# Attention tiles ordered by grid column, value windows loaded one grid row at a time, and four activation casts moved behind key copies

## The chip, the core and the metric

The kernel runs on one core of a Trainium2 chip. A core has a matrix engine (PE, with its weight loads shown apart as PEld), a vector engine (DVE), a scalar engine (ACT), a general engine (POOL) and a queue engine (SP), which work side by side and meet at semaphores. On-chip memory (SBUF) has 128 partitions; PE writes into a smaller memory, PSUM, from which DVE and ACT read. Sixteen DMA engines move data between SBUF and the chip's main memory. DMAs are issued here by SP and, in a few places, by ACT; each of the two works through its list in order, so an issue that has to wait holds up everything behind it.

The metric is the device time of one execution in microseconds (us). The time before is 1057.92 us, the median of three runs between 1056.41 and 1058.7.

## What is computed

One encoder layer over 1024 tokens of 1024 channels in float32. The tokens form a grid of 16 rows and 64 columns. The part that the change touches is the neighbourhood attention: each token attends to a window of 8 rows and 16 columns that is clamped inside the grid, with a learned bias per offset.

```python
h = rms_norm(x, norm1_g[l])
z = h @ w_in[l]
a, gate, q, k, v = jnp.split(z, splits, axis=-1)
conv_out = conformer_conv(a, gate, dw_kernel[l], dw_bias[l], conv_ln_g[l], conv_ln_b[l])
q = rms_norm(q.reshape(B, S, N_HEADS, HEAD_DIM), q_norm_g[l])
k = rms_norm(k.reshape(B, S, N_HEADS, HEAD_DIM), k_norm_g[l])
attn_out = neighbourhood_attention(q, k, v, rpb[l])
x = x + jnp.concatenate([conv_out, attn_out], axis=-1) @ w_out[l]
h = rms_norm(x, norm2_g[l])
x = x + (jax.nn.silu(h @ w_gate[l]) * (h @ w_up[l])) @ w_down[l]
```

There are 8 heads of 64 channels. The convolution has 31 taps over the token positions, for each of 512 channels, then a normalisation over channels and a silu.

## The kernel before

All instructions are written out in Python in the order in which each engine is to run them; no scheduler moves them. The framework adds the semaphore waits that the data need, and gives the SBUF buffers: 22 of kind `G` (128 x 1024), 6 of kind `H` (128 x 4096), 3 of kind `R` (raw weights). PSUM has four banks `mm`, two banks `tp` (mostly for transposes) and a double bank `cv`.

**Products.** A float32 product is made of three matmuls in a reduced format (`mac`, lines 113 to 117): each operand is split into a rounded part (a cast on ACT, line 107) and the rest (a subtraction on DVE or POOL, line 111).

**Start.** The input comes transposed, in two halves of 512 tokens. `h_split` (lines 273 to 277) makes the two parts of one 128-channel block of a half: a cast on ACT (276) and a difference on DVE (277). The keys of the first four tiles of 128 tokens are computed first (`four`, 524 to 528). `head_post` (437 to 445) squares, sums and scales a tile and then puts three entries into the list `woven`: two empty ones and one that does `head_T`. After four tiles the list has twelve entries, with the transposes at places 2, 5, 8 and 11. `weave` takes one entry off that list after each block of three matmuls, so these steps are issued between matmuls of the next product. `head_T` (403 to 413) transposes a scaled tile on PE into a `tp` bank and has ACT copy it out: to `kT` for keys (413), to `qT` for queries (411, two instructions). Between the fourth key tile and the first product of the convolution's gate, `glu_step(0, 0, 0, accs)`, lines 558 and 559 call `h_split` for the blocks 0 to 3 of the second half; lines 562 and 563 call it for the blocks 4 to 7 after that product. The first product that reads the second half is `glu_step(0, 1, 0, accs)` on line 571.

**Middle.** Gate and value of the convolution, the remaining keys and the queries follow; the 31 taps run on DVE (336) with some on ACT and POOL beside PE's products. Meanwhile SP builds six bias tables in main memory (`bias_tables`, 477 to 510), laid out as [i, j, head, column], where i is one of 8 grid rows and j one of 16 columns of a query tile.

**Attention.** A query tile is a block of 8 rows and 16 columns; there are 2 x 4 of them, named by the row half `rh` and the column block `cb`, and a tile's partition is 16 i + j. `order` (617) takes the column blocks 0, 3, 1, 2, each with both halves. Values are written to main memory by token (`value_out`, 417 to 420, issued by ACT). `load_vw` (608 to 613) then loads, for one column block, four grid rows of the columns that its windows can reach (24 or 32) into half of a `G` buffer, so that partition r x columns + c holds row r, column c. Four such loads make a window. `table` (592 to 603) loads a bias table with one partition per query. The loop from line 808 on does two pairs of heads in each of its steps: scores on PE (629), bias and maximum on DVE (641), exponential on ACT (646), scaling on POOL (657), transposes on PE (665), copies on DVE and ACT (670), weighted sums of the values on PE (681). It also issues loads: the table of the middle column blocks for row half 0 at step 4, the window of block 1 at step 6, the table of row half 1 at step 8, the window of block 2 at step 12. Two tables share `H` buffers with older ones. Ahead of the loop stand the windows of blocks 0 and 3 and the last of the first four tables (lines 719 to 728).

SP has eight semaphores for its DMAs and uses them in turn, so an issue also waits until the DMA eight before it has landed.

**After attention.** The output of the convolution is transposed, normalised and split into `cm` by `conv_silu` (777 to 783), where its tokens are put into the order of the attention tiles. From here to the end a tile of 128 tokens is such a block. `rows` (785 to 787) is the view that gives a block's tokens in the input and in the output: `load_x2` (789) loads the residual with it, and `store` (1221 to 1224) writes the result with it. Output projection, norm, and the feed-forward part follow; the latter uses seven products of half-size blocks in place of eight, and its last four partial results are summed on DVE (1246) and stored by ACT's queue.

Of the kernel before, what the change touches and what calls it, by code (L numbers as in the profile page):

```python
# [8 lines left out]
AF = mybir.ActivationFunctionType  # L9
# [15 lines left out]
GW = 64  # L25
# [36 lines left out]
def body(tc, a):  # L62
    from contextlib import ExitStack
    with ExitStack() as ctx:
        build(ctx, tc, a)


def build(ctx, tc, a):
    nc = tc.nc
    pe, act, dve, pool = nc.tensor, nc.scalar, nc.vector, nc.gpsimd  # L70
# [5 lines left out]
    def T(tag, shape, bufs, name, dt=F32):  # L76
        return sb.tile(shape, dt, tag=tag, bufs=bufs, name=name)

    def G(name, dt=F32):
        return T("G", [P, 1024], 22, name, dt)  # L80
# [4 lines left out]
    def H(name, dt=F32):  # L85
        return T("H", [P, 4096], 6, name, dt)
# [13 lines left out]
    def tp(name):  # L100
        return ps.tile([P, 512], F32, tag="tp", bufs=2, name=name)
# [4 lines left out]
    def split(hi, lo, src, sub=(pool,)):  # L106
        act.copy(hi, src)  # L107
        n = src.shape[-1] // len(sub)
        for i, eng in enumerate(sub):
            sl = slice(i * n, (i + 1) * n)  # L110
            eng.tensor_tensor(*[w[..., sl] for w in (lo, src, hi.bitcast(F32))], OP.subtract)  # L111
# [11 lines left out]
    woven = []  # L123
# [94 lines left out]
    FIRST, SECOND, ALL = slice(0, 256), slice(256, 512), slice(0, 512)  # L218
# [33 lines left out]
    for _ in range(11):  # L252
# [3 lines left out]
    qgs = T("qgs", [P, 1], 1, "qgs")  # L256
    dve.tensor_scalar(qgs, qg, HD ** -0.5, None, op0=OP.mult)
    t1 = [dr.tile([NH, 16, 15, ncol], F32, name=f"t1{ty}") for ty, ncol in enumerate((24, 32, 24))]
    tf = {(rh, ty): dr.tile([8, 16, NH, AR * t1[ty].shape[-1]], F32, name=f"tf{rh}{ty}")
          for rh in range(2) for ty in range(3)}  # L260
# [12 lines left out]
    def h_split(h, k, sl):  # L273
        src = xr[h, k // 2][:, k % 2, sl]
        hi, lo = [w[:, k, sl] for w in hT[h]]
        act.activation(hi, src, AF.Copy, scale=g1[:, k:k + 1])
        dve.scalar_tensor_tensor(lo, src, g1[:, k:k + 1], hi.bitcast(F32), OP.mult, OP.subtract)
# [101 lines left out]
    qT, kT = H("qT").rearrange("p (c s) -> p c s", s=S), H("kT").rearrange("p (c s) -> p c s", s=S)  # L379
# [23 lines left out]
    def head_T(n, t, zn):  # L403
        pt = tp(f"zt{n}{t}")
        for c in range(4):
            pe.transpose(pt[:, c * P:(c + 1) * P], zn[:, c * P:(c + 1) * P], ident)
        if n == 0:
            q5 = qT.rearrange("p c (h b i j) -> p c h b i j", h=2, b=4, j=16)
            p5 = pt.rearrange("p (c i b j) -> p c i b j", c=4, i=2, j=16)
            for i in range(2):  # L410
                act.activation(q5[:, :, t // 4, :, 2 * (t % 4) + i, :], p5[:, :, i], AF.Copy, scale=qgs)
        else:
            act.activation(kT[:, :, t * P:(t + 1) * P], pt.rearrange("p (c s) -> p c s", s=P), AF.Copy, scale=kg)

    vd = dr.tile([S, 512], F32, name="vd")
# [21 lines left out]
    def head_post(n, t, z, lag=7):  # L437
        def f(n_taps):
            sd = head_sq(n, t, z)
            pump(2 + {(1, 5): 3, (0, 1): 2}.get((n, t), 0))  # L440
            zn = head_scale(n, t, z, sd)
            pump(1)
            woven.extend([lambda: None] * lag)
            woven.append(lambda: head_T(n, t, zn))
        return f
# [109 lines left out]
    take(1)  # L555
    r_rows(0)
    head_post(1, 3, zs[3], 2)(4)
    for k in range(4):
        h_split(1, k, ALL)
    accs = {}  # L560
    glu_step(0, 0, 0, accs)
    for k in range(4, KB):
# [28 lines left out]

    def table(rh, ty):
        n = AR * t1[ty].shape[-1]
        src = tf[rh, ty].rearrange("i j h c -> (i j) (h c)")
        if rh == 0 and ty == 0:
            parts = [(G(f"tab{k}")[:, :n * min(3, NH - 3 * k)], 3 * k) for k in range(3)]
        else:
            parts = [(H(f"tab{rh}{ty}")[:, :NH * n], 0)]
        heads = []
        for w, h0 in parts:  # L600
            nc.sync.dma_start(w, src[:, h0 * n:h0 * n + w.shape[-1]])
            heads += [w[:, o:o + n] for o in range(0, w.shape[-1], n)]
        return heads


    vwt, vw = {}, {}

    def load_vw(cb, g):
        c0, ncol, _ = WIN[cb]
        if g % 2 == 0:  # L610
            vwt[cb, g // 2] = G(f"vw{cb}{g}").rearrange("p (g d) -> p g d", d=512)
        vw[cb, g] = vwt[cb, g // 2][:4 * ncol, g % 2, :]
        nc.sync.dma_start(vw[cb, g], vd.rearrange("(r c) d -> r c d", c=GW)[g * 4:g * 4 + 4, c0:c0 + ncol, :])


    k4 = kT.rearrange("p c (r w) -> p c r w", w=GW)
# [3 lines left out]
    def score_mm(i):  # L620
        s_, hp = divmod(i, 4)
        rh, cb = order[s_]
        t = rh * 4 + cb
        c0, ncol, _ = WIN[cb]
        s2 = cv(f"s{i}") if i > 0 and i % 2 == 0 else None
        out = []
        for hh in range(2):
            s = (mm(f"s{i}{hh}") if s2 is None else lr(s2)[hh])[:, :AR * ncol]
            pe.matmul(s, qT[hh * HD:(hh + 1) * HD, hp, t * P:(t + 1) * P],  # L629
                      k4[hh * HD:(hh + 1) * HD, hp, rh * 4:rh * 4 + AR, c0:c0 + ncol], start=True, stop=True)  # L630
            out.append(s)
        return out
# [62 lines left out]
    def value(t):  # L695
        z = nat(2, t)
        step(lambda n_taps: (value_out(t, z), pump(n_taps)))
# [1 line left out]
    jobs = []  # L699

    def load_window(cb):
        for g in range(4):
            load_vw(cb, g)

    for t in range(6):
        value(t)
        if t == 2:
            while aside_dma:
                behind()
            tab[0, 0] = table(0, 0)  # L710
        if t == 3:
            tab[1, 0] = table(1, 0)
            tab[0, 3] = table(0, 2)
# [2 lines left out]
    both(0, s0)  # L716
    pump(200)
    value(6)
    for g in range(3):
        load_vw(0, g)  # L720
    s1 = score_mm(1)
    value(7)
    score_norm(0)
    both(1, s1)
    step()
    load_vw(0, 3)
    load_window(3)
    tab[1, 3] = table(1, 2)


    xd = dr.tile([S, D], F32, name="xd")
    cm, x2, xn = [], {}, {}
# [44 lines left out]
    def conv_silu(h, c):  # L777
        y = tp(f"z{h}{c}")
        for i in range(4):
            pe.transpose(y[:, i * P:(i + 1) * P], xh[4 * h + i][:, c * P:(c + 1) * P], ident)  # L780
        act.activation(y, y, AF.Silu, bias=lnb[:, c:c + 1], scale=lng[:, c:c + 1])
        hi, lo = [w[:, c, h * 512:(h + 1) * 512].rearrange("p (b i j) -> p i b j", b=4, j=16) for w in cm]
        split(hi, lo, y.rearrange("p (i b j) -> p i b j", b=4, j=16), (dve,))

    def rows(ap, t):
        rh, cb = divmod(t, 4)
        return ap.rearrange("(h i w) d -> h i w d", h=2, w=GW)[rh, :, cb * 16:cb * 16 + 16, :]

    def load_x2(t):
        x2[t] = G(f"x2{t}")  # L790
        nc.sync.dma_start(x2[t], rows(a["x"], t))
# [16 lines left out]
    for i in range(2, 32 + 2, 2):  # L808
# [5 lines left out]
        if i in (6, 12):  # L814
            load_window(i // 6)
# [60 lines left out]
    proj(4, 0, acc0[4], range(4, 8))  # L876
    act.activation(warm, eps, AF.Silu)
    conv_silu(0, 0)
    proj(5, 0, acc0[5], range(4, 8))
    for t in range(6):  # L880
        load_x2(t)
    later = [(0, c) for c in range(1, 4)] + [(1, c) for c in range(4)]
    woven.extend(lambda q=q: conv_silu(*q) for q in later)
    for ts in (range(4), (4, 5)):
        for k in range(4):
# [335 lines left out]
    def store(p, t, w):  # L1221
        tok, d = {"m2": (0, 0), "m3": (0, 1), "m4": (1, 0), "m7": (1, 1)}[p]
        (nc.scalar if p == "m4" else nc.sync).dma_start(
            rows(a["out"], 4 * tok + t)[:, :, d * 512:(d + 1) * 512], w)
# [34 lines left out]
    for s, p in enumerate(SEQ):  # L1259
        for k in range(QF - 2):  # L1260
            n = s * QF + k
# [34 lines left out]
```

## Time and profile before

| quantity | value |
|---|---|
| median of three runs | 1057.92 us (1056.41 to 1058.7) |
| the profiled execution's own time | 1058.55 us |
| its span, first to last instruction | 1056.8 us |
| mean granted clock of PE | 0.997 |
| data moved by DMA | 144.06 MB, mean 136 GB/s |
| bias and maximum, L641 on DVE | 64 instructions, 497 ns median |
| score matmuls, L629 | 128 instructions, from 223.5 us on |
| value window loads, L613 | 16 |
| table loads, L601 | 8 |
| residual loads, L791 | 8, issued in 593 to 892 ns each |
| output stores, L1223 | 16 |

Durations come from one profiled execution on the chip. A busy PE is not a PE at its peak: matmuls overlap, and those of 128 x 512 are listed with 0.39 us each while they start 0.23 us apart. Names such as `tab<-tf` say what is written and what is read, with the program's buffer names and without numbers. A name with q (SPq, ACTq) is the queue of an engine, which waits, issues DMAs and branches without being busy. In a timeline row stand the start, the length, the engine, the line, the operation and, in brackets, how long the engine was idle before it and what ended that.

### The profile page before, as it was taken

The numbers are of one execution on the slowest core, as the hardware profiler recorded it, in microseconds if no ns is written. First come the engines' busy times: TensorE is split into PE (matmuls) and PEld (weight loads), VectorE is DVE, ScalarE is ACT, GpSimd is POOL, SyncE is SP. The second block draws the span as 40 slices with busy tenths as digits, with TensorE's granted clock in tenths as the row PEclk, the third lists the DMA queues.
The fourth block names the chain that finished last, engine by engine and source line by source line (L and its number), as shares of the span: only waits on it lengthen the run. The fifth ranks groups of instructions, "written<-read, shape, count | busy, mean of one in ns | idle before, by whom it ended". The sixth has DMA issues, their size and how long they took to land.

```text
span 1056.8 us, 14098 instructions
## 1 busy us (share of the span) xinstructions
PE 1044.2 (99%) x5090; PEld 852.8 (81%) x5090; DVE 696.0 (66%) x1048; ACT 452.0 (43%) x987; POOL 382.2 (36%) x301
## 2 busy tenths in 40 slices
PE   9999999999999999999999999999999999999997
PEld 8788888877677887788888888888888888888886
DVE  5788997877665257665564564655656567758883
ACT  6556347737776244532223323232232444433441
POOL 1036765514551302444544445544455200002310
PEclk9999999999999999999999999999999999999999
DMA  9326781245505422133322333232232597634641
GB/s 353 147 62 212 221 256 44 75 152 164 165 26 165 134 100 80 41 109 109 110 100 90 110 113 109 79 130 100 82 133 73 191 327 270 209 100 129 208 130 41
DMA packets 68405, 144.06 MB, mean 136 GB/s; under 512 B 12528, under 2 KB 21232, under 8 KB 67696
## 3 DMA queue, kind: packets, MB, share of 16 engines
q1 hardware_dynamic: 66352, 139.68, 39.4%
q10 hardware_dynamic: 1984, 3.48, 1.0%
q8 instruction: 40, 0.66, 0.3%
q14 instruction: 29, 0.24, 0.1%
HBM read 103.99 MB, written 44.76 MB: 141 GB/s over the span
## 4 chain that ended last, share of the span: by engine, by line
PE 90%; DMA 4%; DVE 2%; ACT 2%; issue 1%; POOL 0%; SPq 0%; ACTq 0%; DVEq 0%; POOLq 0%
PE B L115 6%; PE B L117 6%; PE B L116 6%; PE A L115 4%; PE D L115 4%; PE D L117 4%; PE A L117 4%; PE D L116 4%; PE A L116 4%; PE z L115 3%; PE z L117 3%; PE z L116 3%; DMA tab<-tf 3%; PE gl L115 3%; PE gl L117 3%; PE gl L116 3%
## 5 line engine op out<-in xcount | busy, mean ns | idle before, releaser
L336 DVE SCALAR_TENSOR_TENSOR cv<-u,par,cv 128x1009 f32<-128x1009 f32 (+14 forms) x92 | 117.5, 1277 | 2.3
L362 POOL TENSOR_TENSOR pa<-pa,pr 128x1022 f32<-128x1022 f32 (+5 forms) x24 | 58.0, 2416 | 48.4 <-ACT pr L361 48.0
L107 ACT CAST op<-sr 128x512 fp32r<-128x512 f32 x77 | 47.7, 619 | 51.8 <-PE B2d L117 23.2
L111 DVE TENSOR_TENSOR op<-sr,op 128x512 fp32r<-128x512 f32 x77 | 57.8, 751 | 16.2 <-ACT op L107 16.2
L1079 DVE TENSOR_TENSOR g<-B,g 128x512 f32<-128x512 f32 x22 | 15.2, 691 | 79.1 <-PE B L117 79.1
L1251 POOL TENSOR_TENSOR ou<-ou,resm 128x512 f32<-128x512 f32 x8 | 12.1, 1523 | 144.0 <-DMA resm<-xd 142.2
L1088 ACT ACTIVATE D<-D 128x512 f32<-128x512 f32 x22 | 12.8, 582 | 113.2 <-DVE D L1087 113.2
L1074 DVE TENSOR_TENSOR u<-B,g 128x512 f32<-128x512 f32 x22 | 15.2, 691 | 62.1 <-PE B L117 62.1
L107 ACT CAST op<-wd 128x512 fp32r<-128x512 f32 x66 | 40.9, 619 | 32.1 <-DVE wd L1166 18.2
L935 DVE TENSOR_TENSOR ts<-gu,ts 128x512 f32<-128x512 f32 x44 | 51.0, 1159 | 0.8
L111 DVE TENSOR_TENSOR op<-wd,op 128x512 fp32r<-128x512 f32 x66 | 49.4, 748 | 2.2 <-ACT op L107 0.7
L657 POOL TENSOR_SCALAR e<-e,rs 128x288 f32<-128x288 f32 (+1 forms) x64 | 34.3, 548 | 43.4 <-DVE rs L655 35.5
L1077 ACT ACTIVATE A<-A 128x512 f32<-128x512 f32 x20 | 11.6, 582 | 76.3 <-PE A L117 76.3
L646 ACT ACTIVATE e<-e,mx 128x288 f32<-128x288 f32 (+1 forms) x64 | 36.5, 572 | 17.3 <-DVE mx L641 16.7
L641 DVE CUSTOM_DVE_ANT_0 e<-s,tab 128x288 f32<-128x288 f32 (+1 forms) x64 | 30.7, 499 | 17.8 <-PE s L629 11.2
L935 DVE TENSOR_TENSOR ts<-gu 128x512 f32<-128x512 f32 x22 | 34.0, 1547 | 0.0
L665 PEld LDWEIGHTS p<-ident,e 128*96 128x96 f32 (+1 forms) x192 | 20.4, 136 | 14.4 <-issue 8.7
L665 PE MATMUL p<-ident,e 128*96 128x128 f32 (+1 forms) x192 | 28.9, 286 | 3.1 <-POOL e L657 3.1
L389 ACT ACTIVATE sq<-z,r 128x64 f32<-128x64 f32 x96 | 28.6, 334 | 4.7 <-PE z L117 4.7
L361 ACT ACTIVATE pr<-u,par 128x1022 f32<-128x1022 f32 (+5 forms) x24 | 27.0, 1137 | 1.6 <-ACT vs L419 1.6
L986 POOL TENSOR_TENSOR xn<-xn,xn 128x512 f32<-128x512 f32 x4 | 6.9, 1725 | 57.0 <-DVE sn L986 53.6
L115 PE MATMUL B2d<-op 128*128 128x512 f32 x66 | 25.8, 391 | 0.0
(1040 smaller groups left out, 3469.3 us busy)
## 6 DMA issues: line engine op xcount, KB each, us to landing
gu<-in_gu SPq DMA_DIRECT2D x44, 512.0 KB
sr<-sd SPq DMA_DIRECT2D x77, 256.0 KB
sd<-sd SPq DMA_DIRECT2D x22, 512.0 KB
wd<-in_wd SPq DMA_DIRECT2D x44, 256.0 KB
sd<-g SPq DMA_DIRECT2D x33, 256.0 KB
x<-in_x SPq DMA_DIRECT2D x16, 512.0 KB
xd<-x SPq DMA_DIRECT2D x8, 512.0 KB
resm<-xd SPq DMA_DIRECT2D x16, 256.0 KB
```

The source lines that it names most:

```text
L107: act.copy(hi, src)
L111: eng.tensor_tensor(*[w[..., sl] for w in (lo, src, hi.bitcast(F32))], OP.subtract)
L115: pe.matmul(acc, lh, rh, start=start, stop=False, skip_group_check=True)
L116: pe.matmul(acc, lh, rl, start=False, stop=False, skip_group_check=True)
L117: pe.matmul(acc, ll, rh, start=False, stop=stop, skip_group_check=True)
L336: dve.scalar_tensor_tensor(acc[:, o], uc[:, i], dwk[:, c, t:t + 1], acc[:, o], OP.mult, OP.add)
L362: pool.tensor_tensor(pa[:, o], pa[:, o], pr[:, o], OP.add)
L641: dve.tensor_tensor_reduce(out=es[i][:, hh], in0=s[hh], in1=tab[rh, cb][2 * hp + hh], scale=-1.0, scalar=3.0e38, op0=OP.add, op1=OP.min, a ...
L646: act.activation(e, e, AF.Exp, bias=mx.pop((i, hh)), scale=-1.0, accum_out=sums[i][:, hh:hh + 1])
L657: pool.tensor_scalar(es[i][:, hh], es[i][:, hh], rs[:, hh:hh + 1], 1.0, op0=OP.mult, op1=OP.mult)
L665: pe.transpose(pt[:m, g * P:(g + 1) * P], es[i][:, hh, g * m:(g + 1) * m], ident)
L935: dve.tensor_tensor(o, l, r, OP.subtract)
```

## The change

Four things change.

Within an attention tile the tokens go by column: a token's partition is 8 j + i in place of 16 i + j. The query copies, the split of the convolution's output, the table loads and the view `rows` follow that order; the tables in main memory stay as they were.

A value window is loaded by one DMA for each of its four grid rows, and where two halves of a buffer are loaded together, one DMA takes that row for both. Where there were 16 loads there are 36: 12 for column block 0, whose last two parts still come apart, and 8 for each other block.

The four calls of `h_split` ahead of `glu_step(0, 0, 0, accs)` become entries of `woven`: blocks 0 and 1 right behind the first key tile's transposes and copy, blocks 2 and 3 right behind the second's.

```diff
         if n == 0:
-            q5 = qT.rearrange("p c (h b i j) -> p c h b i j", h=2, b=4, j=16)
+            q5 = qT.rearrange("p c (h b j i) -> p c h b j i", h=2, b=4, j=16)
             p5 = pt.rearrange("p (c i b j) -> p c i b j", c=4, i=2, j=16)
             for i in range(2):
-                act.activation(q5[:, :, t // 4, :, 2 * (t % 4) + i, :], p5[:, :, i], AF.Copy, scale=qgs)
+                act.activation(q5[:, :, t // 4, :, :, 2 * (t % 4) + i], p5[:, :, i], AF.Copy, scale=qgs)
...
     head_post(1, 3, zs[3], 2)(4)
-    for k in range(4):
-        h_split(1, k, ALL)
+    for at_, k in zip((3, 4, 6, 7), range(4)):
+        woven[at_] = lambda k=k: h_split(1, k, ALL)
     accs = {}
     glu_step(0, 0, 0, accs)
...
-        src = tf[rh, ty].rearrange("i j h c -> (i j) (h c)")
+        src = tf[rh, ty].rearrange("i j h c -> j i (h c)")
...
-            nc.sync.dma_start(w, src[:, h0 * n:h0 * n + w.shape[-1]])
+            nc.sync.dma_start(w, src[:, :, h0 * n:h0 * n + w.shape[-1]])
...
-    def load_vw(cb, g):
+    def load_vw(cb, *gs):
         c0, ncol, _ = WIN[cb]
-        if g % 2 == 0:
-            vwt[cb, g // 2] = G(f"vw{cb}{g}").rearrange("p (g d) -> p g d", d=512)
-        vw[cb, g] = vwt[cb, g // 2][:4 * ncol, g % 2, :]
-        nc.sync.dma_start(vw[cb, g], vd.rearrange("(r c) d -> r c d", c=GW)[g * 4:g * 4 + 4, c0:c0 + ncol, :])
+        if gs[0] % 2 == 0:
+            vwt[cb, gs[0] // 2] = G(f"vw{cb}{gs[0]}").rearrange("p (g d) -> p g d", d=512)
+        w = vwt[cb, gs[0] // 2]
+        for r in range(4):
+            nc.sync.dma_start(w[r * ncol:(r + 1) * ncol, gs[0] % 2:gs[-1] % 2 + 1, :],
+                              vd.rearrange("(g r c) d -> r c g d", r=4, c=GW)[r, c0:c0 + ncol, gs[0]:gs[-1] + 1, :])
+        for g in gs:
+            vw[cb, g] = w[:4 * ncol, g % 2, :]
...
     def load_window(cb):
-        for g in range(4):
-            load_vw(cb, g)
+        load_vw(cb, 0, 1)
+        load_vw(cb, 2, 3)
...
-    for g in range(3):
-        load_vw(0, g)
+    load_vw(0, 0, 1)
+    load_vw(0, 2)
...
-        hi, lo = [w[:, c, h * 512:(h + 1) * 512].rearrange("p (b i j) -> p i b j", b=4, j=16) for w in cm]
+        hi, lo = [w[:, c, h * 512:(h + 1) * 512].rearrange("p (b j i) -> p i b j", b=4, j=16) for w in cm]
...
     def rows(ap, t):
         rh, cb = divmod(t, 4)
-        return ap.rearrange("(h i w) d -> h i w d", h=2, w=GW)[rh, :, cb * 16:cb * 16 + 16, :]
+        return ap.rearrange("(h i w) d -> h w i d", h=2, w=GW)[rh, cb * 16:cb * 16 + 16, :, :]
```

## The prediction

> **What bounds the kernel now.** I read the busy shares of the page first, then the waits of TensorE (PE), the chain of waits that ended last, and the timelines where that chain leaves PE.
>
> ```profile
> span 1056.8 us, 14098 instructions
> PE 1044.2 (99%) x5090; PEld 852.8 (81%) x5090; DVE 696.0 (66%) x1048; ACT 452.0 (43%) x987; POOL 382.2 (36%) x301
> PE p L665 <- POOL e L657: 3.1, 3, 2.2
> PE zt L406 <- ACT kT L413: 1.0, 1, 1.0
> ```
>
> PE is busy 1044.2 of 1056.8 us, and its two large waits are the last two rows. A change that removes no PE work can win only in such holes, in slow-clock stretches, and in the ends. The change touches three of them: the hole of 1.0 us (first key tiles), the 3.1 us in attention, and the end, where stores follow the last sum.
>
> **Attention.** The chain of waits between 242 and 283 us (start, length, what) consists almost wholly of two table loads; VectorE (DVE) adds the tables to the scores and waits for both.
>
> ```profile
> 242.75 15.79 DMA tab<-tf
> 261.57 16.97 DMA tab<-tf
> ```
>
> Why does a table take 16 us? These are the sizes of the loads, and busy times by stretch (PE, PEld, DVE, ACT, POOL, clock, share of the 16 DMA engines, GB/s):
>
> ```profile
> tab<-tf SPq DMA_DIRECT2D x3, 1152.0 KB
> tab<-tf SPq DMA_DIRECT2D x2, 1536.0 KB
> vw<-vd SPq DMA_DIRECT2D x8, 256.0 KB
> vw<-vd SPq DMA_DIRECT2D x8, 192.0 KB
> 213.50:217.00 3.50, 3.50 (x17) 2.90 (x16) 3.40 (x3) 1.15 (x1) 1.92 (x1) 1.00 0.91 334
> 222.50:225.50 3.00, 3.00 (x15) 1.97 (x14) 2.89 (x4) 0.00 (x0) 0.00 (x0) 1.00 0.26 101
> 278.50:280.50 2.00, 0.00 (x0) 0.00 (x0) 1.80 (x8) 1.14 (x4) 0.48 (x1) 1.00 0.26 99
> 282.40:285.80 3.40, 3.40 (x16) 1.88 (x14) 2.25 (x8) 1.72 (x6) 2.24 (x4) 0.50 0.58 156
> 1051.00:1055.00 4.00, 0.00 (x0) 0.00 (x0) 0.23 (x1) 0.00 (x0) 0.00 (x0) 0.85 0.51 168
> ```
>
> The first stretch is nearly all table loading: 0.91 of the engines, 334 GB/s. In the second and third only value windows move: 0.26, which is 4 engines of 16. The last has output stores alone: 0.51, 8 of 16. The first index of the transfer explains it: a value load walks 4 grid rows, a store 8, a table 128. So a quarter of each table, the part on those four engines, queues behind all value loads asked for earlier, while the other twelve idle.
>
> What the two late tables cost PE is read from the starts of the score matmuls, one group per loop step:
>
> ```profile
> 252.24 1.24 PE L629 MATMUL s<-kT,qT 64*128 64x288 f32 x8
> 256.45 1.24 PE L629 MATMUL s<-kT,qT 64*128 64x288 f32 x8
> 261.32 1.24 PE L629 MATMUL s<-kT,qT 64*128 64x288 f32 x8
> 270.07 1.56 PE L629 MATMUL s<-kT,qT 64*128 64x384 f32 x8
> 274.64 1.56 PE L629 MATMUL s<-kT,qT 64*128 64x384 f32 x8
> 281.70 2.31 PE L629 MATMUL s<-kT,qT 64*128 64x384 f32 x8
> 287.84 1.56 PE L629 MATMUL s<-kT,qT 64*128 64x384 f32 x8
> ```
>
> The undisturbed steps are 4.21 (252.24 to 256.45) and 4.57 us (270.07 to 274.64). The step at 256.45 took 4.87, the one at 274.64 took 7.06, the next 6.14: losses of 0.66, 2.49 and 1.57. The last one has no hole: the stretch 282.40 to 285.80 ran at clock 0.50, after the hole. **Attention loses 4.7 us.**
>
> If value loads use 12 to 16 engines, are the tables on time? From the landing of the last value tile SP has ahead of the first late table:
>
> ```profile
> 237.02 0.33 ACTq L420 DMA_DIRECT2D vd<-vs  x1
> 239.11 3.60 SPq L613 DMA_DIRECT2D vw<-vd  x5
> ```
>
> Five loads now, 4 + 8 = 12 after, at 0.6 us each if an issue stays at that: the table goes out at 239.1 + 7.2 = 246.3, minus 1.0 by which all is earlier (below): 245.3. It is 1.18 MB, 3.5 us at 334 GB/s, and I add 1.76 us for latency (the vd store's issue ends at 237.35, the load that waits for it starts at 239.11): 250.6. It is needed with the scores of 256.45, at about 255.9 after the shift. The second late table (1.57 MB) has 8 value loads and another table ahead of it: 6.35 MB in all since 239.1, 19 us at 334 GB/s, so its bytes are through by 259.9 with the latency, and I allow 265 for SP's waits on earlier landings; it is needed at 273.4 (274.64, plus 0.5 for the matmuls, minus the 1.0 and 0.66 gained before it). The spare time runs out only below some 190 GB/s (6.35 MB in 33.5 us). I take the whole 4.7. The 20 additional issues (about 12 us of SP) lie under SP's waits; queued behind them are these two tables and the output weights, which PE needs after attention.
>
> The table's own pattern changes from 128 rows in order to 16 times 8. An issue of such a form is the 0.6 of the value loads; with the transfer at half speed, 167 GB/s throughout, the first table still arrives in time and the second 2.6 us late: this is rival 2.
>
> Each value buffer now has up to eight landings to wait for, not two. A wait of PE's queue with nothing to wait for costs this much (ns, min/median/max):
>
> ```profile
> L1292 PEldq EVENT_SEMAPHORE x2: 51/51/51, 1056.3 to 1056.7; - x2
> ```
>
> Bounds: nothing, or 20 more of them in front of PE, 1.0 us. I take 0.3, since the undisturbed steps above have such waits already and keep their pace.
>
> [...]
>
> **The start.** Casts of the second half (L276) sit in ScalarE's (ACT's) queue ahead of the copies of the first key tiles:
>
> ```profile
> 34.08 2.55 ACT L276 ACTIVATE hT<-xt,par 128x512 fp32r<-128x512 f32 x4
> 36.53 1.24 ACT L413 ACTIVATE kT<-zt,par 128x512 f32<-128x512 f32 x2
> 37.25 0.66 PE L406 MATMUL zt<-ident,zn 128*128 128x128 f32 x4 [1.04 <-ACT kT L413]
> 43.03 0.39 PE L115 MATMUL gl<-hT,ag10h 128*128 128x512 f32 x1
> ```
>
> The third tile's transposes need one of two PSUM buffers. After: copy at 34.08, two casts, copy, two casts; the first copy is done at 34.7, PE wants the buffer at 36.2. Gain 1.04, and 0.06 of the slow restart: **1.1 us**. The eight casts and two copies end together at the same time as before, 40.3 (37.77 and four casts more), DVE's difference follows each cast, and the first reader of the first one starts at 43.03, then 42.0: no new wait. The shift survives up to attention if DVE, the busiest engine beside PE there, shifts too; it waited shortly before attention for work that follows PE's, so it does, and I pass the gain on whole. Bounds 0 and 1.1.
>
> ```profile
> 199.42 0.20 DVE L397 RECIPROCAL r<-d 128x8 f32<-128x8 f32 x1 [1.04 <-ACT d L392]
> ```
>
> **The end.**
>
> ```profile
> 1047.18 4.69 ACTq L1223 DMA_DIRECT2D out_dram<-ou  x4
> 1050.54 0.69 DVE L1246 TENSOR_TENSOR ou<-A3d,ou 128x512 f32<-128x512 f32 x1 [0.67 <-PE A3d L117]
> out_dram<-ou ACTq DMA_DIRECT2D x4, 256.0 KB
> 1055.00:1056.70 1.70, 0.00 (x0) 0.00 (x0) 0.00 (x0) 0.00 (x0) 0.00 (x0) 0.50 0.12 46
> ```
>
> Four stores of 0.26 MB at 168 GB/s take 1.56 us each and come 1.36 us apart, so they back up; the last bytes move at about 1055.4 (0.12 x 1.7 x 16 / 8 = 0.4 us into the last stretch) and are reported some tenths later. On 16 engines there is no backlog: issue ends 1051.87, plus the 1.76 us of the vd store (256 KB, 128 rows): 1053.6. Against 1055.4 to 1055.9 this is 1.8 to 2.3; I take **2.1 us**. The rest of the page's end stays.
>
> **Strided writes.** Query copies (L411) and the split of the convolution's output (L107, L111) now write single elements 32 bytes apart instead of runs of 16.
>
> ```profile
> L411 ACT ACTIVATE qT<-zt,qgs x16: 467/472/477, 160.3 to 202.1; 128x256 f32<-128x256 f32 x16
> L107 ACT CAST cm<-z x8: 587/587/588, 331.4 to 346.3; 128x512 fp32r<-128x512 f32 x8
> L107 ACT CAST h<-t x8: 575/587/590, 390.9 to 410.8; 128x512 fp32r<-128x512 f32 x8
> 332.01 0.69 DVE L111 TENSOR_TENSOR cm<-z,cm 128x512 fp32r<-128x512 f32 x1 [1.76 <-ACT cm L107]
> 332.76 0.50 PE L117 MATMUL pj<-wo,cm 128*128 128x512 f32 x1
> 336.56 0.50 PE L117 MATMUL pj<-wo,cm 128*128 128x512 f32 x1
> ```
>
> Runs of 16 (cm) cost what whole rows (h) cost, 587 ns; single elements are not in the trace. Bounds: nothing, or twice the time. The query copies are covered even then: 0.47 us more in each of 16, on an engine that is 43% busy, and the scores come six value projections later. The split is not: PE waits for it at 332.76 and 336.56, so doubling costs 2 x (0.59 + 0.69) = 2.6 us. I take 0.6, nearer to the lower end by the rows of 587. [...]
>
> The residual's loads by columns change from 8 to 16 engines; PE waits for none of them now. Nothing is charged.
>
> **Sum.** -1.1 -4.7 -2.1 +0.3 +0.6 = -7.0 us, against the profiled execution's 1058.55 (its span is 1056.8): 1051.6. It lies 0.6 above the median of the runs, 1057.92, from which the same sum gives **1050.9**, the forecast.
>
> **Rivals.**
> 1. Forecast: 1050.9. Chance 0.60.
> 2. The tables stay late, because rate or pattern keeps the loads under 190 GB/s. For it: the slice rates of attention are far below 334. Against: these are the rates of four full engines. 1057.92 - 1.1 - 2.1 + 0.9 = 1055.6. Chance 0.14.
> 3. Strided writes double: 1050.9 + 2.0 = 1052.9. Chance 0.13.
> 4. Slower: rows of one buffer wait for each other's landing, since four loads now write one tile. Price 0.6 + 1.76 = 2.36 us per wait: ahead of the first late table nine waits and three free issues, so it goes out at 238.1 + 21.2 + 1.8 = 261.1 and lands (3.5 + 1.76) at 266.4, 10.5 late, plus 1.6 of slow clock; the second then is just in time. -7.0 + 12.1 = +5.1: 1063.0. A wait adds 1.76 and 5.3 us are spare, so the table is late from the fourth on, and the gain is gone from about the sixth. Against it: the five loads in 3.60 us above include two halves of one buffer, without such a wait; but those are columns, not partitions. Chance 0.08.
> 5. The loads and stores stay on as few engines as before: only the start gains: 1057.1, no change. Chance 0.05.
>
> **Numbers.** No change can be told within 0.2%, 2.1 us. Cases 1 to 3 are faster by more: 0.87; case 5 is the same: 0.05; case 4 slower: 0.08. Range: all gains at their larger bound and no cost is 1057.92 - 1.1 - 4.7 - 2.3 = 1049.8, minus 1.5, by which the lowest run lies under the median: 1048.3. The upper end takes in case 2: 1056.0; cases 4 and 5 stay out.
>
> **What would show it.** Right: no hole before the third key tile at about 36 us; the DMA share over 0.6 while value windows load; no DVE wait for tables and score steps of 4.2 and 4.6 us throughout, with no stretch at clock 0.50 before the end; last stores near 1.0 share; the span about 3.5 us behind the last DVE sum. Wrong: table loads still 10 us or longer in the chain of waits; the casts and differences of cm above 0.8 us; row loads more than 2 us apart on SP.

## The result, and the profile after

| | before | after |
|---|---|---|
| median of six runs each (us) | 1058.01 (1056.41 to 1058.70) | 1053.38 (1053.25 to 1053.70) |
| profiled execution, its own time (us) | 1058.55 | 1053.70 |
| its span (us) | 1056.8 | 1052.0 |
| mean granted clock of PE | 0.997 | 0.999 |

The ratio after to before is 0.9958, with a 95% interval of 0.9945 to 0.9971. The change gains 4.6 us, where the prediction had 7.0. The time lies within the predicted range, but nearer to its rival 3 (1052.9) than to its forecast (1050.9). The runs after also lie closer together: within 0.45 us, against 2.3 before.

First the busy shares from the page of the changed kernel, and then four of its seven rows of PE's waits (total, times, longest, us):

```profile
PE 1042.6 (99%) x5090; PEld 851.6 (81%) x5090; DVE 699.9 (67%) x1048; ACT 458.6 (44%) x987; POOL 380.9 (36%) x301
```

```profile
PE pj L117 <- DVE cm L111: 0.9, 2, 0.5
PE pj L115 <- ACT cm L107: 0.7, 2, 0.5
PE gl L115 <- DVE zn L399: 0.6, 1, 0.6
PE p L669 <- POOL e L661: 0.4, 1, 0.4
```

The wait of 1.0 us before the third key tile is not among them, and that of 3.1 us in attention is down to 0.4. In their place stand 1.6 us of waits for `cm`.

To say where the 4.8 us of span came from, take the starts of three instructions that both kernels have, in the timelines of PE. Before:

```profile
223.46 0.76 PE L629 MATMUL s<-kT,qT 64*128 64x288 f32 x4
331.64 0.39 PE L117 MATMUL pj<-wo,at 128*128 128x512 f32 x1
1050.11 0.39 PE L117 MATMUL A3d<-op 128*128 128x512 f32 x1
```

After:

```profile
222.59 0.76 PE L633 MATMUL s<-kT,qT 64*128 64x288 f32 x4
325.99 0.39 PE L117 MATMUL pj<-wo,at 128*128 128x512 f32 x1
1046.92 0.39 PE L117 MATMUL A3d<-op 128*128 128x512 f32 x1
```

These are the first scores, the last product of the first block's projection with an attention operand (just ahead of the first with `cm`), and the last matmul of all. They come 0.87, 5.65 and 3.19 us earlier than before; the span ends 4.8 earlier. So the start gave 0.87, attention 5.65 - 0.87 = 4.78, everything from the first use of `cm` to the last matmul took back 5.65 - 3.19 = 2.46, and the end gave 4.8 - 3.19 = 1.6.

**Attention.** Score matmuls of the changed kernel:

```profile
251.36 1.24 PE L633 MATMUL s<-kT,qT 64*128 64x288 f32 x8
255.57 1.24 PE L633 MATMUL s<-kT,qT 64*128 64x288 f32 x8
259.79 1.24 PE L633 MATMUL s<-kT,qT 64*128 64x288 f32 x8
268.54 1.56 PE L633 MATMUL s<-kT,qT 64*128 64x384 f32 x8
273.10 1.56 PE L633 MATMUL s<-kT,qT 64*128 64x384 f32 x8
```

The steps are 4.21 and 4.56 us, as the undisturbed ones were, also in the rows between and around these. There is no half-clock stretch either: the granted clock is 1.00 from 243 to 275, from 275 to 290 and from 290 to 330 us. But the margin was small. SP's queue, a stretch of the transfers (columns as in the prediction), and the first use of the last table on DVE:

```profile
225.52 17.98 SPq L614 DMA_DIRECT2D vw<-vd  x18
243.60 1.17 SPq L601 DMA_DIRECT2D tab<-tf  x2
244.82 14.74 SPq L614 DMA_DIRECT2D vw<-vd  x8
259.65 0.52 SPq L601 DMA_DIRECT2D tab<-tf  x1
```

```profile
213.50:217.00 3.50, 3.50 (x17) 2.92 (x16) 3.39 (x4) 0.56 (x1) 2.39 (x1) 1.00 0.98 234
243.00:275.00 32.00, 32.00 (x321) 23.46 (x321) 23.47 (x91) 26.68 (x81) 16.20 (x32) 1.00 0.98 215
```

```profile
274.16 0.56 DVE L645 CUSTOM_DVE_ANT_0 e<-s,tab 128x384 f32<-128x384 f32 x1 [0.72 <-PE s L633]
```

All 16 engines are busy now (0.98 from 243 to 275 us, 0.63 before), yet they move 215 GB/s (187 before). The stretch in which tables move almost alone fell from 334 to 234 GB/s while its share rose from 0.91 to 0.98: with the pattern of 16 times 8 the engines were busy longer for fewer bytes. DVE's first use of the last table waits for the scores, not for the table. How much was spare shows in SP's queue. Since SP uses its eight semaphores in turn, the eighth issue behind a table waits for that table's landing. Behind the last table this is the last value load. The 36 value loads (issue times in ns, first and last start) and two rows of SP's waits for them:

```profile
L614 SPq DMA_DIRECT2D vw<-vd x36: 289/342/1626, 212.8 to 272.3; - x36
```

```profile
SPq L614 <- DMA tab<-tf: 17.6, 3, 7.7
SPq L614 <- DMA vw<-vd: 3.1, 6, 1.0
```

Three value loads waited for a table, one for each of the three tables. The last of them went out at 272.3, when the last table had landed: 1.9 us before DVE used it at 274.16.

**The split.** The casts and differences of `cm`, by shape (ns, min/median/max), with the query copies:

```profile
L107 ACT CAST cm<-z x8: 1101/1141/1200, 325.7 to 343.2; 128x512 fp32r<-128x512 f32 x8
L111 DVE TENSOR_TENSOR cm<-z,cm x8: 1148/1188/1241, 326.9 to 344.5; 128x512 fp32r<-128x512 f32 x8
L411 ACT ACTIVATE qT<-zt,qgs x16: 732/778/792, 159.4 to 201.4; 128x256 f32<-128x256 f32 x16
```

587 ns became 1141, 0.69 us became 1.19, and 472 ns became 778. The PE timeline shows what the first two cost:

```profile
326.89 0.50 PE L115 MATMUL pj<-wo,cm 128*128 128x512 f32 x1 [0.52 <-ACT cm L107]
328.09 0.50 PE L117 MATMUL pj<-wo,cm 128*128 128x512 f32 x1 [0.46 <-DVE cm L111]
331.71 0.50 PE L115 MATMUL pj<-wo,cm 128*128 128x512 f32 x1 [0.17 <-ACT cm L107]
332.90 0.50 PE L117 MATMUL pj<-wo,cm 128*128 128x512 f32 x1 [0.45 <-DVE cm L111]
```

These waits are 1.6 of the 2.46 us. From the last product with an attention operand to the last of these four the changed kernel takes 332.90 - 325.99 = 6.91 us, the kernel before 336.56 - 331.64 = 4.92 us, so this stretch lost 2.0 in all. The remaining 0.5 lies before two of the following transposes, whose weight loads on PEld wait until a difference has read the PSUM bank that they will overwrite:

```profile
337.80 0.42 PEld L784 LDWEIGHTS z<-ident,xh 128*128 128x128 f32 x4 [0.49 <-DVE cm L111]
341.75 0.42 PEld L784 LDWEIGHTS z<-ident,xh 128*128 128x128 f32 x4 [0.51 <-DVE cm L111]
```

**Start and end.** The third key tile's transposes have no wait:

```profile
36.45 0.60 PE L406 MATMUL zt<-ident,zn 128*128 128x128 f32 x4
```

The last stores, the last sum, and a stretch of the stores alone:

```profile
1043.99 4.63 ACTq L1227 DMA_DIRECT2D out_dram<-ou  x4
1047.35 0.69 DVE L1250 TENSOR_TENSOR ou<-A3d,ou 128x512 f32<-128x512 f32 x1 [0.67 <-PE A3d L117]
```

```profile
1048.00:1050.00 2.00, 0.00 (x0) 0.00 (x0) 0.04 (x1) 0.00 (x0) 0.00 (x0) 0.97 0.80 193
```

The span ends 1052.0 - 1048.04 = 4.0 us behind the last sum; before, it was 1056.8 - 1051.23 = 5.6. The prediction had 3.5 in mind. The stores' share of the engines is 0.80, against 0.51 before; the prediction had named a share near 1.0 as a sign, which was not reached.

### The profile page after: what moved, and what is told of

Same layout as the page of the kernel before. It is cut to its first block, busy times and chain, and to the rows that moved or that the text cites. A ratio compares the mean times of both kernels' runs of the same rounds, so it can differ in the third digit from the quotient of the medians.

```text
span 1052.0 us, 14155 instructions
## 1 busy us (share of the span) xinstructions
PE 1042.6 (99%) x5090; PEld 851.6 (81%) x5090; DVE 699.9 (67%) x1048; ACT 458.6 (44%) x987; POOL 380.9 (36%) x301
## 4 chain that ended last, share of the span: by engine, by line
PE 93%; DVE 2%; ACT 2%; DMA 1%; issue 0%; SPq 0%; POOL 0%; ACTq 0%; DVEq 0%; POOLq 0%
PE B L115 6%; PE B L117 6%; PE B L116 6%; PE A L115 4%; PE A L116 4%; PE D L117 4%; PE D L116 4%; PE D L115 4%; PE A L117 4%; PE z L115 4%; PE z L117 3%; PE z L116 3%; PE gl L115 3%; PE gl L117 3%; PE gl L116 3%; PE p L669 2%
```

## The experiments

The theory after the result had four parts: the moved casts win about 1 us; the row loads win attention by spreading over all engines; the column order wins at the last stores and loses at the strided split; and the pattern of the table loads is slow but hidden. The rivals were that attention gained from the column order rather than from the rows, and that something other than the strided writes took the 2.5 us. Runs were made on several chips, and each is compared with the kernel before on its own chip: its median there was 1057.54 for the moved casts, the row loads, the column order and the contiguous split, 1058.41 for the loads of two rows, and 1058.38 for the other four.

**One part at a time.** First the moved casts alone: the kernel before with this.

```diff
-    for k in range(4):
-        h_split(1, k, ALL)
+    for at_, k in zip((3, 4, 6, 7), range(4)):
+        woven[at_] = lambda k=k: h_split(1, k, ALL)
```

> Before with the four casts moved behind the key copies, nothing else. If the parts of the change add up (theory A), PE's hole of 1.04 us at the third key tile goes and the time falls by 0.8 to 1.1 us; attention, the split of the convolution's output and the end stay as before. If the gain at the start is given back until attention (rival), the time stays within 0.3 us of before.

Measured: 1056.71 us (1055.05 to 1059.04, eleven runs), ratio 0.999 [0.9981, 0.9998]: -0.8 us. The wait before the third key tile is gone. Its profiled execution was one of the shortest (1055.55), and the reason lies in attention: there is a hole of PE, but the stretch behind it runs at full clock.

```profile
276.00:279.00 3.00, 0.42 (x8) 0.17 (x4) 1.82 (x8) 1.16 (x4) 0.50 (x1) 1.00 0.25 97
279.00:283.00 4.00, 3.85 (x30) 2.48 (x32) 3.59 (x14) 3.56 (x11) 2.95 (x6) 1.00 0.63 181
```

So a similar hole came with the slow clock in the kernel before (0.50) and without it here (1.00). This fits the scatter of the versions that keep the holes: of the eleven runs of the column order with reordered tables (below), the three with a mean clock of 1.000 took 1057.65 to 1057.96 us, the eight with 0.997 or 0.998 took 1058.98 to 1059.72. That it makes the whole scatter of the kernel before is not shown. The versions without the holes scatter by 0.3 to 1.4 us, those with them that have five runs or more by 2.0 to 4.0.

Then the row loads alone: the kernel before with the new `load_vw` and `load_window` and nothing else.

```diff
-        nc.sync.dma_start(vw[cb, g], vd.rearrange("(r c) d -> r c d", c=GW)[g * 4:g * 4 + 4, c0:c0 + ncol, :])
...
+        for r in range(4):
+            nc.sync.dma_start(w[r * ncol:(r + 1) * ncol, gs[0] % 2:gs[-1] % 2 + 1, :],
+                              vd.rearrange("(g r c) d -> r c g d", r=4, c=GW)[r, c0:c0 + ncol, gs[0]:gs[-1] + 1, :])
```

> Before with the values loaded row by row, tokens and tables in the old order. Theory A (value loads held four DMA engines, the tables queued behind them): no table on the chain of waits, no stretch at half clock, 4.7 to 4.8 us faster, cm casts still 587 ns, stores as before. Rival B (the tables came in time because of their own new pattern): attention keeps its holes and the time stays within 1 us of before.

Measured: 1053.72 us (1053.47 to 1054.55, five runs), ratio 0.9963 [0.995, 0.9975]: -3.8 us, less than the 4.7 expected, which the interval still takes in. Attention is clean, and the tables keep their rate:

```profile
213.50:217.00 3.50, 3.50 (x17) 2.88 (x16) 3.43 (x3) 1.12 (x1) 2.23 (x1) 1.00 0.88 346
243.00:275.00 32.00, 32.00 (x322) 23.42 (x319) 23.21 (x89) 26.36 (x80) 16.42 (x32) 1.00 0.74 229
```

In the second stretch more bytes move than in the changed kernel (229 against 215 GB/s), at a share of 0.74 in place of 0.98. The wait at the third key tile stays (0.8 us in its waits).

Then the column order alone: the kernel before with the new query copies, table loads, split of `cm` and `rows`.

```diff
-        src = tf[rh, ty].rearrange("i j h c -> (i j) (h c)")
+        src = tf[rh, ty].rearrange("i j h c -> j i (h c)")
...
-        hi, lo = [w[:, c, h * 512:(h + 1) * 512].rearrange("p (b i j) -> p i b j", b=4, j=16) for w in cm]
+        hi, lo = [w[:, c, h * 512:(h + 1) * 512].rearrange("p (b j i) -> p i b j", b=4, j=16) for w in cm]
```

> Before with the tokens by column alone: query copies, table loads, the split of the convolution's output, residual loads and stores; value loads and casts as before. Theory A: the two late tables stay (holes of 0.4 and 2.2 us, half clock), cm casts and differences near 1140 and 1190 ns cost 2.5 us, the stores win 1.6 us: 0.9 us slower than before. Rival B: the tables are in time, 3.9 us faster than before.

Measured: 1065.14 us (1062.76 to 1065.34, five runs), ratio 1.0065 [1.0052, 1.0077]: +7.6 us, a clear miss of the expectation. Its stretches show the slow tables and two stretches at half clock:

```profile
213.50:217.00 3.50, 3.50 (x17) 2.89 (x16) 3.39 (x4) 1.25 (x2) 1.70 (x1) 1.00 0.88 176
264.40:267.80 3.40, 3.40 (x14) 1.86 (x13) 2.20 (x11) 1.99 (x7) 1.07 (x3) 0.50 0.25 94
288.30:291.70 3.40, 3.40 (x16) 1.80 (x14) 2.25 (x8) 1.68 (x6) 2.28 (x4) 0.50 0.64 171
```

and its chain of waits has both late tables, later than before:

```profile
243.00 19.22 DMA tab<-tf
265.27 19.21 DMA tab<-tf
```

While the value loads have a quarter of the engines (0.26 from 260.2 to 264.4 us), the tables are on the path, and there their pattern costs: in the first stretch 176 GB/s against 334 at about the same share (0.88 and 0.91). The parts thus do not add up: -0.8 - 3.8 + 7.6 = +3.0, and the whole gives -4.6. The column order is only cheap behind the row loads.

**Is it the pattern of the tables?** The column order alone again, but with the tables stored in main memory in the order in which they are now read, so that a load is 128 rows in order:

```diff
-        src = tf[rh, ty].rearrange("i j h c -> j i (h c)")
+        src = tf[rh, ty].rearrange("j i h c -> (j i) (h c)")
```

> The kernel with the column order alone (1065.14), and the tables laid out in main memory as [j, i, head, column], so that a table load is again 128 rows in order. Theory D (loading 16 times 8 rows halves the rate of a table, 176 against 334 GB/s): the first table loads run over 300 GB/s again, attention loses what it lost before (4 to 5 us, not 10), and the time falls by about 6 us to 1059. If the order by column itself slows attention, the time stays at 1065.

Measured: 1059.07 us (1057.65 to 1059.72, eleven runs), ratio 1.0006 [0.9998, 1.0015]. The tables are back at their rate and at about their length in the chain of waits before; the two views one after the other:

```profile
213.50:217.00 3.50, 3.50 (x17) 2.88 (x17) 3.42 (x3) 1.13 (x1) 2.23 (x1) 1.00 0.88 348
```

```profile
242.55 15.41 DMA tab<-tf
261.05 17.68 DMA tab<-tf
```

By the medians 6.1 of the 7.6 us were the tables' pattern, by the differences to each one's own runs of the kernel before 6.9. What is left of the column order, +0.7, is about the strided split less the gain at the stores (2.5 - 1.6).

**Does attention need the row loads, or only early tables?** The kernel before, with its loads on four engines, but with each late table asked for ahead of the value loads that stood in front of it.

```diff
+    tab[1, 3] = table(1, 2)
     load_vw(0, 3)
     load_window(3)
-    tab[1, 3] = table(1, 2)
...
-            if i in (6, 12):
-                load_window(i // 6)
+            if i in (8, 12):
+                load_window(1 if i == 8 else 2)
```

> Before with two table loads asked for earlier on SP: the last of the first four tables ahead of the value loads that follow the last value tile, and the table of row half 1 ahead of the window of block 1, which moves from step 6 to step 8. Value loads stay on four engines. Theory A (a table is late only because a quarter of it queues behind value loads): both tables land within 8 us, the holes of 0.4 and 2.2 us and the half clock go, about 4 us faster than before, near 1053.5. If late tables are a matter of the whole load's rate (rival), the holes stay and the time is that of before.

Measured: 1054.23 us (1053.41 to 1054.82, five runs), ratio 0.9961 [0.9949, 0.9974]: -4.1 us. The value loads still have a quarter of the engines, and PE's wait in attention is down to the 0.4 of the changed kernel all the same (a stretch, then the waits of PE):

```profile
222.50:225.50 3.00, 3.00 (x15) 1.96 (x14) 2.93 (x3) 0.00 (x0) 0.00 (x0) 1.00 0.26 98
```

```profile
PE p L665 <- POOL e L657: 0.4, 1, 0.4
```

One part of the expectation failed: only the first of the two tables landed within 8 us. The last packet of the second moves at 267.3 us, 18.7 us after its issue at 248.6; value loads and another table stood ahead of it. It was early all the same, as DVE uses it from 276.05 on. The intervals of this and of the row loads alone overlap. What attention lost was the queueing of a part of each table behind the value loads; sending the tables first does as much as making the loads faster.

**Is it the first index that sets the number of engines?** The kernel before, with each value load cut into two of two grid rows each.

```diff
+        for r in (0, 2):
+            nc.sync.dma_start(vw[cb, g][r * ncol:(r + 2) * ncol], vd.rearrange("(r c) d -> r c d", c=GW)[g * 4 + r:g * 4 + r + 2, c0:c0 + ncol, :])
```

> Before with each value load cut into two of two grid rows, all else as before. If the first index of a transfer sets how many DMA engines it uses (theory A), these loads use two engines: a share of 0.13 while they move alone, twice the queue on those two, the tables later still, 10 us or more slower than before. If cutting the loads in itself is what helped, it is faster than before.

Measured: 1077.54 us (two runs), against 1058.41, ratio 1.0185 [1.0155, 1.0214]: +19 us.

```profile
222.50:225.50 3.00, 3.00 (x15) 1.94 (x15) 2.93 (x3) 0.00 (x0) 0.00 (x0) 1.00 0.13 51
```

Two rows, 0.13: two engines of 16, where four rows had 0.26 and eight rows 0.51. Cutting a load was of no use by itself: the share went down with the first index of each piece.

**The strided split.** The changed kernel, but the split writes whole runs and the strided side is the read from PSUM (elements 256 bytes apart).

```diff
-        hi, lo = [w[:, c, h * 512:(h + 1) * 512].rearrange("p (b j i) -> p i b j", b=4, j=16) for w in cm]
-        split(hi, lo, y.rearrange("p (i b j) -> p i b j", b=4, j=16), (dve,))
+        hi, lo = [w[:, c, h * 512:(h + 1) * 512].rearrange("p (w i) -> p w i", i=8) for w in cm]
+        split(hi, lo, y.rearrange("p (i w) -> p w i", i=8), (dve,))
```

> After with the split of the convolution's output written in order and read from PSUM with a stride (64 elements), the same values in the same places. If what costs is the write of single elements 32 bytes apart (theory A), the casts of cm fall to about 590 ns and the differences to about 690, PE's four waits for them go, and the time is 2.5 us under after, about 1050.9. Rival C: a strided side costs the same wherever it is; then casts and differences stay over 1000 ns and the time stays that of after.

Measured: 1050.82 us (1050.58 to 1051.35, five runs), ratio 0.9936 [0.9922, 0.9949].

```profile
L107 ACT CAST cm<-z x8: 586/586/589, 325.2 to 340.2; 128x512 fp32r<-128x512 f32 x8
L111 DVE TENSOR_TENSOR cm<-z,cm x8: 691/692/693, 325.8 to 340.8; 128x512 fp32r<-128x512 f32 x8
```

Both are back at their old durations, PE has no wait for `cm` left, and the median lies 2.6 us below that of the changed kernel (2.1 where each is taken against its own runs of the kernel before, which scatter more); the alignment above has 2.46. The write side alone makes the cost; the strided read of PSUM shows none here. This version is faster than both kernels.

**What the column order is worth.** The changed kernel without its column order, which is the kernel before with the moved casts and the row loads.

> After without the order by column: row loads and the moved casts, tokens in the old order. If parts add up: 4.6 us (start and attention) under before, near 1052.9; against the version that reads with a stride (1050.82) it lacks the stores on 16 engines alone, 1.7 us by the traces. If the column order wins more than its stores, it is over 1053.5.

Measured: 1052.64 us (1052.42 to 1053.54, five runs), ratio 0.995 [0.9938, 0.9962]. By the medians that is 0.7 us better than the changed kernel, by the differences to their own runs of the kernel before 1.1: as it was made, the column order costs more at the split than it wins at the stores. In the last stretch its stores have half the engines again:

```profile
1047.00:1050.00 3.00, 0.00 (x0) 0.00 (x0) 0.00 (x0) 0.00 (x0) 0.00 (x0) 1.00 0.51 177
```

**Both repairs.** The changed kernel with the contiguous split and with the tables stored in the order of their reading (the two diffs above together).

> The version that reads with a stride (1050.82), with the tables laid out as [j, i, head, column]. Tables have time to spare there, so theory A and D expect the same time within 0.5 us, with table loads again over 300 GB/s. If slow tables still held back the value loads behind them in a way that costs, it is 1 us or more faster.

Measured: 1050.77 us (1050.51 to 1050.85, five runs), ratio 0.9929 [0.9915, 0.9943]. By the medians this equals the contiguous split alone, although the tables move fast:

```profile
213.50:217.00 3.50, 3.50 (x17) 2.92 (x16) 3.39 (x4) 0.30 (x2) 2.39 (x1) 1.00 1.02 389
```

By the differences to their own runs of the kernel before it is 0.9 us better, which the overlapping intervals do not tell from nothing. So behind the row loads the tables' pattern is hidden as far as these runs can tell. Against the run before this one, which was made on the same chip, the column order with a cheap split and reordered tables is worth 1.9 us, near the 1.6 that the end shows.

## Why the prediction was right, and where not

**The start, 1.1: about right.** The row of the third key tile is 0.80 us earlier and shows no wait; the moved casts alone gave 0.8. In the profile after, another wait, that for `zn` (0.6 us, 0.2 before), stands ahead of it and takes back 0.4; this wait is between nothing and 1.2 us in the profiles of the experiments, with or without the moved casts, so it does not belong to the change. The gain survived up to attention (0.87 us at the first scores), as was argued.

**Attention, 4.7: right, 4.78 in the profiles.** By the medians of runs the row loads alone gave 3.8 and the tables first 4.1. The mechanism was shown from both sides: a faster way for the value loads (229 GB/s from 243 to 275 us with the row loads alone, 187 before), and tables ahead of slow value loads, each remove the loss, while two engines per load (0.13) make it far worse (1077.54 us). The first table went out at 243.60, where 245.3 was forecast, since an issue of a row load takes 0.34 us in the median, not 0.6. The transfers were slower than taken for it: the last table landed at 272.3, where the forecast had 259.9 and allowed 265. The two errors had opposite signs, and of the spare time 1.9 us were left. That the whole gain came was in part luck.

**Rival 2 had its mechanism right, and a small margin kept it off.** The half-rate pattern that it names is real: 176 GB/s in the column order alone, 334 before. It did not bind, but only by the 1.9 us above. Its threshold of 190 GB/s cannot be set beside the 215 of the stretch, which counts bytes of other loads too. Of the whole prediction this was the thinnest margin, and the chance of 0.14 was not too high.

**The strided writes, 0.6: the step that failed.** This term was mis-sized; it was 2.5. The rows of 587 ns, of runs of 16 elements, were taken as the nearest, and the value was put near the lower bound. But the changed writes have no runs at all, and the upper bound of 2.6, of doubled durations, which was the author's estimate, was met almost exactly (1141 against 587, 1188 against 692). The mechanism of rival 3 is what happened, and its time, 1052.9, is near the measured one. The prediction had named casts and differences of `cm` above 0.8 us as a sign that it was wrong, and they were. Other distances between the elements were not run, so how the cost depends on them is not shown. The query copies slowed down too, by 0.3 us each (778 against 472 ns), and were hidden as argued.

**The end, 2.1: 1.6.** The backlog of stores is gone as argued. The size was off: the last issue ends at 1043.99 + 4.63 = 1048.62, and the span 3.4 us behind it. Before, these were 4.9 us, and a gain of 2.1 needed 2.8. The last store landed 2.3 us after its issue (SP's wait for it ends at 1050.9), not the 1.76 us that were taken over from the store of `vd`. That store walks 128 rows in order, these walk 16 times 8; whether this is the reason was not tried.

**Additional waits for landings, 0.3: nothing to see.** The score steps are 4.21 and 4.56 us, as the undisturbed ones were before. The prediction called two of PE's waits its large ones; its list has a third of 1.0 us, for `ones` at the start, which is the same in both kernels.

By terms: -0.9 - 4.8 + 2.5 - 1.6 = -4.8 in the profiled spans, against -1.1 - 4.7 + 0.6 - 2.1 + 0.3 = -7.0. Of the 2.2 us between them, 1.9 are the strided writes. Rivals 4 and 5 are excluded. SP's waits for landings of value loads add up to 3.1 us, the longest 1.0, where rival 4 had 1.76 for each load; and the transfers of attention fill the engines (0.98). Some row loads were more than 2 us apart, which the prediction had named as a sign of rival 4, but there SP waited for a table eight issues back or for values on their way to main memory.

What stays open is why a table load of 16 times 8 rows was slower than one of 128 rows in order (176 against 348 GB/s, both at a share of 0.88). No run separates its possible causes.

## What to carry to other kernels

Look at the share of the DMA engines while one kind of load moves alone: where it is a plain fraction such as 0.13, 0.26 or 0.51, the first index of that transfer may be too small, and whatever is queued behind it on those engines is late too; either make that index larger or send the urgent transfer first. The share alone does not settle it: with the row loads alone it was 0.29 between 222.5 and 225.5 us too, and no stretch shown here has row loads filling the engines by themselves. Halving the index did: loads of two rows had 0.13 in place of 0.26. When a layout changes, price every write whose innermost run becomes a single element by its upper bound (here 1141 ns in place of 587), and see whether the stride can be moved to the side that reads PSUM (here 586 ns). Parts of a change that share a resource are not additive: here one part alone cost 7.6 us and, behind another that made room for it, about 1.

## What the runs showed of the hardware that was not expected

- The busy share of the 16 DMA engines followed the first index of the transfer: 0.13 for 2 (loads of two rows), 0.26 for 4 (value loads before) and 0.51 for 8 (output stores before).
- A load of 128 partitions that is written as 16 times 8 moved 176 GB/s at a share of 0.88 (column order alone) and 234 at 0.98 (the changed kernel), where 128 rows in order moved 346 to 348 at 0.88.
- Writing single float32 elements 32 bytes apart took ACT 1141 ns in place of 587 and DVE 1188 in place of 692 for 512 elements per partition; reading PSUM with elements 256 bytes apart took 586 and 692.
- A hole of PE was not always followed by the half clock. A stretch of 3.4 us at 0.50 followed holes whose wait was 2.2 us (before), 3.9 and 3.0 us (column order alone), while in the moved casts alone a hole with a wait of 2.7 us was followed by full clock. With loads of two rows, after a hole whose wait of 10.5 us ended at 299.19, the clock was still 0.50 here:

```profile
300.00:304.00 4.00, 4.00 (x14) 1.99 (x13) 2.38 (x9) 2.26 (x8) 2.08 (x4) 0.50 0.14 53
```
